# A hybrid layer with 32 experts: the sums of five and six of its modulations as products on TensorE

## The chip, the cores and the metric

The kernel runs on one core of a Trainium2 chip. The metric is the device time of one execution in microseconds (us); lower is better. TensorE (PE in the profile) does matrix products, VectorE (DVE) and ScalarE (ACT) work along the rows of a tile of 128 partitions, GpSimd (POOL) does the same in part, and SyncE (SP) issues transfers from the chip's memory (HBM).

## The reference, cut to what matters

One layer on 256 tokens of width 1024. A conditioning vector `c` gives six vectors of 1024, the modulations; two of them shift and scale the input of the mixers, the third scales the mixers' result, the other three do the same around the experts:

```python
mods = silu(c) @ w_ada + b_ada                 # [1024] @ [1024, 6144], float32
shift1, scale1, gate1, shift2, scale2, gate2 = split(mods, 6)
h = rms_norm(x, norm1_g) * (1 + scale1) + shift1
proj = h @ w_in
y_rwkv = rwkv7_time_mix(proj[..., :RWKV_PROJ], ...)     # 8 heads, recurrent
y_moba = moba_attention(proj[..., RWKV_PROJ:], ...)     # 8 heads, causal
x = x + gate1 * (concat(y_rwkv, y_moba) @ w_out)
h = rms_norm(x, norm2_g) * (1 + scale2) + shift2
y = moe_ffn(h, w_router, ..., w_gate_up, b_gate_up, w_down, b_down)   # top 4 of 32 experts
return x + gate2 * y
```

The expert weights are 32 times 12.58 MB, 403 of the 451 MB that the kernel reads.

## The kernel before, in words

Everything up to the experts is written as threads (generators): the input's norm, the projections, the two mixers, the output projection, the routing, the loads, and `t_mods`, which this change touches. `mix.run` steps them in an order written out by hand as a string of letters (`_ORDER`), one letter per step; a step runs from one `yield` to the next. So the program order on each engine is the order of the steps, and each engine does its instructions in that order. The change leaves the string as it is, and `t_mods` keeps its number of steps.

Weights come in through one list of loads, issued on SP's queue in a fixed order (`_STREAM`), each into a half of one of twelve 2 MB tiles (`take`, `done`, `release`). A load waits in SP's queue until the half that it was given has been read by its former users, and the loads behind it wait with it. `need` gives a thread the half that a load filled, `done` gives it back.

The first two modulations (shift1, scale1) are made earlier on TensorE, at line 557, four column blocks of 512 in four groups of 32 partitions of one PSUM bank (`pa`). `t_mods` makes the other four, in two rounds. Round `g=1` makes gate1 and shift2, `g=2` makes scale2 and gate2. Each round takes eight pieces of w_ada, one per 128 rows of the matrix, 128 partitions by 2048 columns (1 MB). Before, VectorE multiplies each piece by that piece's 128 values of silu(c), one per partition (`sc`), and adds it to an accumulator of 128x2048 (1 MB, half a tile), in two instructions of 1024 columns (lines 1144 and 1146). The 128 partitions are summed at the end by TensorE: `pcol` turns 1024 of the columns into a column layout (line 1154), for s2 at line 1156 and A2 at line 1164, and `pg` spreads the gate over all partitions (line 1185). GpSimd clears the gate's half of the accumulator first (line 1134), and its first partition gets the bias.

Names that follow: `pm`, `pk`, `pr`, `pv`, `plo` are the projections (line 196; line 191 splits a weight for them on VectorE), `px` and `pz` the low-rank parts (686, 706). In the recurrent mixer, `pz2a` and `pz2b` (line 845) and `px2a` and `px2b` (856) are the steps of a triangular solve; between them VectorE evacuates PSUM at lines 848 and 860. `pgu` (line 1395) is the first product of an expert, `pga` (1357) gathers its tokens, `pz` at line 1421 is its second product.

Of the kernel before, what the change touches and what calls it, by code (L numbers as in the profile page):

```python
# [24 lines left out]
AF = mybir.ActivationFunctionType  # L25
ALU = mybir.AluOpType
# [3 lines left out]
D = 1024  # L30
T = 256
KC = 8
# [95 lines left out]
def body(ctx, tc, cst, x, c, w_ada, b_ada, norm1_g, w_in, rwkv_mu, rwkv_w0, rwkv_w_up, rwkv_a0, rwkv_a_up, rwkv_g_up,  # L128
         rwkv_k_k, rwkv_k_a, rwkv_r_k, rwkv_ln_g, rwkv_ln_b, q_norm_g, k_norm_g, w_out, norm2_g, w_router, b_router,
         w_gate_up, b_gate_up, w_down, b_down, out, dbg=None, stop=99):  # L130
    nc = tc.nc
    mm = nc.tensor.matmul
    tr = nc.tensor.transpose
    act = nc.scalar.activation
    V = nc.vector
    G = nc.gpsimd
# [20 lines left out]
    def U(name, wide=False, kind="f"):  # L157
        e = find(wide, kind)
        assert e is not None, (name, [x[1:] for x in live])
        if e == ():  # L160
            nsl[0] += 1
            e = [up.tile([128, 4096], F32, name=f"u{nsl[0]}_" + (name if isinstance(name, str) else "_".join(str(z) for z in name)), tag="u"), kind, [None, None]]
            live.append(e)
        if wide:
            e[2] = [name, name]
            return e[0]
        i = e[2].index(None)
        e[2][i] = name
        return e[0][:, i * 2048:(i + 1) * 2048]

    def release(name):
        for e in live:
            if name in e[2]:
                e[2] = [None if x == name else x for x in e[2]]
                if e[2] == [None, None]:
                    live.remove(e)
                return
        raise KeyError(name)

    def S2(name, dims=None):  # L180
        t = sm.tile([128, 512], F32, name=name, tag="s2", bufs=8)
        return t

    def PB(name):
        return pp.tile([128, 512], F32, name=name, tag="B", bufs=8)
# [16 lines left out]
    def dram(ap, offset, dims):  # L202
        return bass.AP(tensor=ap.tensor, offset=ap.offset + offset, ap=dims)
# [16 lines left out]
    def cc(name, lo=0, n=None):  # L220
        o, w = _CST[name]
        b = o + lo
        e = o + (w if n is None else lo + n)
        return CK[:, b:e] if o < NKEEP else CH[:, b - NKEEP:e - NKEEP]

    ident = cc("ident")
    ones = cc("ones")
# [202 lines left out]
    def pump():  # L430
        while S["wmax"] and S["next"] < len(plan) and fits(S["halves"]) and held[0] + plan[S["next"]][2] <= S["wmax"]:
            load_next()
# [16 lines left out]
    def done(name):  # L449
        t = W.pop(name)  # L450
        if name[0] in ("gu", "dn"):
            held[0] -= 2
            for h in range(2):
                if any((name, h) in e[2] for e in live):
                    release((name, h))
        else:
            held[0] -= 1
            release(name)
        pump()

    def need(name):
        while name not in W or S["next"] < len(plan) and name == plan[S["next"]][0]:
            assert fits(), ("no slot", name, H, list(W))
            load_next()
        return W[name]

    def take(name, kind="f", wide=False):
        assert name not in H
        H.add(name)
        return U(name, wide, kind)  # L470

    def drop(*names):
        for n in names:
            H.remove(n)
            release(n)
        pump()
# [16 lines left out]
    sc = cp.tile([128, KC], F32, name="sc")  # L493
# [17 lines left out]
    def pairs(t, a, r):  # L511

        return t.rearrange("p (a q r) -> p a r q", a=4, r=2)[:, a, r, :]
# [612 lines left out]
    g2z = cp.tile([128, D], F32, name="g2z")  # L1126

    def t_mods():
        GA = None
        for g in (1, 2):  # L1130
            yield "slots", 1
            a = take(f"acc{g}")
            gate = slice((g - 1) * 1024, g * 1024)
            G.memset(a[:, gate], 0.0)
            yield
            nc.sync.dma_start(out=a[0:1, gate], in_=dram(b_ada, (2 if g == 1 else 5) * D, [[D, 1], [1, D]]))
            yield
            for k in range(KC):
                yield "unit", ("ada", g, k)
                w = need(("ada", g, k))  # L1140
                for n in range(2):
                    o = slice(n * 1024, (n + 1) * 1024)
                    if k == 0 and n != g - 1:
                        V.tensor_scalar(a[:, o], w[:, o], sc[:, 0:1], None, op0=ALU.mult)
                    else:
                        V.scalar_tensor_tensor(a[:, o], w[:, o], sc[:, k:k + 1], a[:, o], op0=ALU.mult, op1=ALU.add)  # L1146
                    if n == 0:
                        yield
                done(("ada", g, k))
            yield  # L1150
            ps = PB("pcol")
            o = 1024 if g == 1 else 0
            for k in range(KC):
                mm(ps[:, k:k + 1], pairs(a[:, o:o + 1024], k // 2, k % 2), ones, start=True, stop=True)
            if g == 1:
                V.tensor_tensor(out=s2, in0=ps[:, 0:8], in1=p2[:, 0:8], op=ALU.add)
                GA = a.rearrange("p (a n) -> p a n", a=2)
                E_["g1"] = GA[:, 0]
                for d in range(2):
                    for i in range(2):  # L1160
                        nc.sync.dma_start(out=GA[64 * d + 32 * i:64 * d + 32 * i + 32, 1].rearrange("p (j n) -> p j n", j=2),
                                          in_=dram(b_gate_up, i * 512, [[2 * D, 32], [D, 2], [1, 512]]))
            else:
                V.scalar_tensor_tensor(A2, ps[:, 0:8], 1.0, p2[:, 8:16], op0=ALU.add, op1=ALU.add)
                V.scalar_tensor_tensor(A2, A2, math.sqrt(D), p2[:, 16:24], op0=ALU.mult, op1=ALU.mult)

                tw = S2("tw")[:, 0:KC * NE].rearrange("p (k e) -> p k e", k=KC)
                sw = S2("sw")[:, 0:NE]
                V.tensor_tensor(out=tw, in0=wr, in1=s2[:, :, None].to_broadcast([128, KC, NE]), op=ALU.mult)
                V.tensor_reduce(out=sw, in_=tw.rearrange("p k e -> p e k"), axis=AX.X, op=ALU.add)  # L1170
                V.tensor_tensor(out=wr, in0=wr, in1=A2[:, :, None].to_broadcast([128, KC, NE]), op=ALU.mult)
                bg = cp.tile([128, 1024], F32, name="bgu", tag="bgu")
                E_["bgu"] = bg.rearrange("p (j n) -> p j n", j=2)
                act(bg.bitcast(F32R), GA[:, 1], AF.Copy)
                V.tensor_tensor(out=bg[64:128].bitcast(F32R), in0=GA[64:128, 1], in1=bg[64:128], op=ALU.subtract)
                V.tensor_tensor(out=pick, in0=ident[:, 0:64], in1=ident[:, 64:128], op=ALU.add)
                yield
                ps = PB("psw")
                mm(ps[:, 0:NE], ones.to_broadcast([128, 128]), sw, start=True, stop=True)
                V.tensor_tensor(out=br, in0=ps[:, 0:NE], in1=br, op=ALU.add)  # L1180
            yield
            for n in range(2):
                o = n * 512 if g == 1 else 1024 + n * 512
                ps = PB("pg1")
                mm(ps, ones.to_broadcast([128, 128]), a[:, o:o + 512], start=True, stop=True)
                act(GA[:, 0, n * 512:(n + 1) * 512] if g == 1 else g2z[:, n * 512:(n + 1) * 512], ps, AF.Copy)
                yield
            if g == 2:
                drop("acc2")
            yield "set", f"mod{g}"  # L1190

    def t_out():
# [371 lines left out]
    class Solo:  # L1564
# [6 lines left out]
        def down(self, b, j):  # L1571
# [4 lines left out]
            if j % 4 == 3:  # L1576
                done(("dn", e, j // 4))

    mix.run({"a": t_input(), "b": t_project(), "c": t_mods(), "d": t_rwkv(), "e": t_values(), "f": t_finish(), "g": t_moba(), "h": t_att(0),
             "i": t_att(1), "j": t_out(), "k": t_rank(), "l": t_split(), ".": t_load()}, _ORDER, early)  # L1580
    if stop <= 1:
# [6 lines left out]
    for pair in range(NE // 2):  # L1588
# [6 lines left out]
        for b in range(2):  # L1595
# [4 lines left out]
            t, i, g = XG[e]  # L1600
# [73 lines left out]
    for n in range(2):  # L1674
        for t in range(2):
            ps = PB("pcb")
# [25 lines left out]
```

## Time and profile before

| | us |
|---|---|
| median of 3 runs (lowest, highest) | 1211.56 (1210.47, 1213.37) |
| the profiled execution | 1214.2 |
| its span in the profile | 1212.1 |
| PE busy | 1126.8 (93%) |
| DVE busy | 383.3 (32%) |
| ACT busy | 173.9 (14%) |
| POOL busy | 52.5 (4%) |
| read from HBM | 449.31 MB, 372 GB/s over the span |

The mean granted clock of TensorE is 0.969 of full speed. Busy shares are means over stages with different limits, so the table says little on a change in one stage; the rows below are by stage. Some matmul records can be missing, and the end of a matmul is modelled.

### The profile page before, as it was taken

Reading aid. Unit: us, or ns where it says so; the run is one execution under the profiler, and the core shown is the slowest. Engines: PE = TensorE matmul, PEld = TensorE weight load, DVE = VectorE, ACT = ScalarE, POOL = GpSimd, SP = SyncE. Lnnn points to the kernel's source line nnn. Section 1 sums busy time; section 2 is a strip of 40 time slices with the busy share of each in tenths; the row PEclk is TensorE's granted clock in tenths of the full one; section 3 lists DMA queues with packets and bytes.
Section 4 is the critical chain, followed back from the end, with each engine's and each line's share of the span. In section 5 each row is a group of like instructions: output and inputs, shape, how many; then the busy total and the mean of one; then the engine's idle time right before and its main releaser. Section 6 shows DMA issues by size and latency. Waiting matters only on the chain.

```text
span 1212.1 us, 13675 instructions
## 1 busy us (share of the span) xinstructions
PE 1126.8 (93%) x5769; PEld 495.5 (41%) x5769; DVE 383.3 (32%) x739; ACT 173.9 (14%) x321; POOL 52.5 (4%) x74
## 2 busy tenths in 40 slices
PE   5999888989999999999989998998999899988998
PEld 3776676544433333343234333432343333333332
DVE  2379998552112222220213021212121212111213
ACT  3356354221100000010001000100010000000000
POOL 0002440010000000000000000000000000000000
PEclk9999877998999999999899999999999999999999
DMA  8796573577999999999999999999999999999994
GB/s 284 243 336 237 194 230 121 177 326 312 336 367 417 424 426 429 427 429 425 426 426 429 427 428 428 427 428 427 428 427 428 428 428 428 427 427 428 427 429 203
DMA packets 55436, 451.31 MB, mean 372 GB/s; under 512 B 7738, under 2 KB 17160, under 8 KB 25802
## 3 DMA queue, kind: packets, MB, share of 16 engines
q1 hardware_dynamic: 55082, 449.85, 90.7%
q8 instruction: 48, 0.79, 0.3%
q10 hardware_dynamic: 288, 0.52, 0.1%
q14 instruction: 18, 0.15, 0.0%
HBM read 449.31 MB, written 1.05 MB: 372 GB/s over the span
## 4 chain that ended last, share of the span: by engine, by line
PE 55%; DMA 35%; DVE 7%; issue 1%; ACT 1%; SPq 0%; POOL 0%; ACTq 0%; DVEq 0%; POOLq 0%
PE pgu L1395 22%; PE pz L1421 9%; PE pga L1357 5%; DMA u_('dn', 11, 1)_0_3596<-in_w_down 3%; DMA u_('dn', 19, 1)_0_4783<-in_w_down 3%; DMA u_('dn', 27, 1)_0_5609<-in_w_down 3%; DMA u_('dn', 23, 1)_0_5196<-in_w_down 3%; DMA u_('dn', 15, 1)_0_4370<-in_w_down 3%; DMA u_('dn', 29, 1)_0_5812<-in_w_down 3%; PE pcb L1430 3%; DMA u_('gu', 27, 3)_0_5506<-in_w_gate_up 3%; DMA u_('gu', 11, 3)_0_3483<-in_w_gate_up 3%; DMA u_('gu', 23, 3)_0_5093<-in_w_gate_up 3%; DMA u_('gu', 19, 3)_0_4680<-in_w_gate_up 3%; DMA u_('dn', 7, 1)_0_3169<-in_w_down 2%; DMA u_ada<-in_w_ada 2%
## 5 line engine op out<-in xcount | busy, mean ns | idle before, releaser
L1401 ACT ACTIVATE gt<-gt 128x512 f32<-128x512 f32 x32 | 20.2, 630 | 492.0 <-DVE gt L1400 491.9
L1400 DVE TENSOR_SCALAR gt<-pgu 128x512 f32<-128x512 f32 x32 | 22.1, 692 | 179.3 <-PE pgu L1395 179.3
L1375 DVE COPY ct<-pct 128x256 f32<-128x256 f32 x17 | 7.2, 425 | 222.7 <-PE pct L1374 222.7
L1357 PE MATMUL pga<-oh,u_ada 128*128 128x256 f32 (+1 forms) x288 | 74.6, 382 | 0.4 <-DVE oh L1350 0.2
L1433 DVE TENSOR_TENSOR u_x<-pcb,u_x 128x512 f32<-128x512 f32 x60 | 41.5, 692 | 98.5 <-PE pcb L1430 98.5
L1357 PEld LDWEIGHTS pga<-oh,u_ada 128*128 128x128 f32 x288 | 50.4, 201 | 49.5 <-issue 45.2
L1430 PE MATMUL pcb<-z,ct 128*128 128x512 f32 x120 | 59.5, 618 | 0.0
L1412 ACT ACTIVATE at<-pat 128x512 f32<-128x512 f32 x32 | 19.1, 597 | 230.2 <-PE pat L1410 230.2
L1380 POOL CAST sel<-pick 128x128 fp32r<-128x128 f32 x32 | 9.6, 301 | 853.5 <-PE pz L1421 521.7
L1426 DVE TENSOR_TENSOR z<-pz,g2z 128x512 f32<-128x512 f32 x30 | 20.8, 692 | 74.4 <-PE pz L1421 74.4
L1361 DVE TENSOR_SCALAR u_ada<-pga,A,s 128x256 f32<-128x256 f32 (+1 forms) x24 | 12.0, 499 | 86.3 <-PE pga L1357 86.3
L1430 PEld LDWEIGHTS pcb<-z,ct 128*128 128x128 f32 x120 | 20.3, 189 | 38.7 <-issue 38.7
L1395 PE MATMUL pgu<-u_ada,u_ada 128*64 128x512 f32 x112 | 28.7, 635 | 0.0
L1410 PEld LDWEIGHTS pat<-cst_k,ut 128*128 128x128 f32 x128 | 17.9, 209 | 26.0 <-issue 13.0
L1388 PE MATMUL pgu<-bgu,sel 128*128 128x512 f32 x64 | 25.0, 472 | 2.8 <-PEq L1455 2.8
L196 PE MATMUL pm<-u_wmq,u_hs 128*128 128x512 f32 x96 | 24.9, 415 | 2.3 <-DVE u_wmq L191 2.3
L1359 ACT ACTIVATE u_ada<-pga,s,A 128x256 f32<-128x256 f32 (+1 forms) x24 | 12.7, 528 | 89.7 <-PE pga L1357 89.6
L1402 DVE TENSOR_SCALAR ut<-pgu 128x512 f32<-128x512 f32 x32 | 22.1, 692 | 5.9 <-PE pgu L1395 5.1
L1410 PE MATMUL pat<-cst_k,ut 128*128 128x128 f32 x128 | 23.9, 310 | 0.0
L1403 DVE SCALAR_TENSOR_TENSOR ut<-ut,gt 128x512 f32<-128x512 f32 x32 | 22.2, 692 | 4.7 <-ACT gt L1401 1.2
L196 PEld LDWEIGHTS pm<-u_wmq,u_hs 128*128 128x128 f32 x96 | 18.9, 200 | 7.5 <-DVE u_wmq L191 2.8
L1146 DVE SCALAR_TENSOR_TENSOR u_krg<-u_ada,sc,u_krg 128x1024 f32<-128x1024 f32 x13 | 20.4, 1581 | 0.2
(717 smaller groups left out, 2094.1 us busy)
## 6 DMA issues: line engine op xcount, KB each, us to landing
u_ada<-in_w_gate_up SPq DMA_DIRECT2D x16, 1024.0 KB
u_ada<-in_w_ada SPq DMA_DIRECT2D x13, 1024.0 KB
u_ada<-in_w_ada SPq DMA_DIRECT2D x24, 256.0 KB
u_ada<-in_w_in SPq DMA_DIRECT2D x6, 1024.0 KB
u_sa<-in_w_gate_up SPq DMA_DIRECT2D x5, 1024.0 KB
u_ada<-in_w_down SPq DMA_DIRECT2D x5, 1024.0 KB
u_lo<-in_w_in SPq DMA_DIRECT2D x4, 1024.0 KB
u_vk<-in_w_gate_up SPq DMA_DIRECT2D x3, 1024.0 KB
```

What stands on the lines that cost most here:

```text
L196: mm(out, a[p].bitcast(F32R), b[q_].bitcast(F32R), start=start and i == 0, stop=stop and i == 2, **kw)
L1357: mm(ps[:, 0:n], pairs(xn2[:, t, :], k // 2, k % 2), oh[:, t, 0:n], start=(t == 0), stop=(t == 1))
L1388: mm(ps[a], s_, E_["bgu"][:, a, :].bitcast(F32R), start=True, stop=False, skip_group_check=True)
L1395: mm(ps[a][hs[h], :], xl(k), w[:, a * 1024 + h * 512:a * 1024 + (h + 1) * 512], start=False, stop=(k == KC - 1), skip_group_check=True)
L1400: V.tensor_scalar(gt, ps[0], 7.0, None, op0=ALU.min)
L1402: V.tensor_scalar(ut, ps[1], 7.0, -7.0, op0=ALU.min, op1=ALU.max)
L1403: V.scalar_tensor_tensor(ut, ut, 1.0, gt, op0=ALU.add, op1=ALU.mult)
L1410: tr(pt[:, f * 128:(f + 1) * 128], ut.rearrange("p (q r) -> p r q", r=4)[:, f], ident)
L1421: mm(pz[n][hs[b], :], at[:, j % 4, j // 4, :], w[b][:, n * 512:(n + 1) * 512], start=(j == 0), stop=(j == KC - 1), skip_group_check=True)
L1426: V.tensor_tensor(out=z[i][0:n], in0=pz[i][0:n], in1=g2z[0:n, i * 512:(i + 1) * 512], op=ALU.mult)
L1430: mm(ps[i], ct[0:n, t * 128:(t + 1) * 128], z[i][0:n], start=True, stop=True)
L1433: V.tensor_tensor(out=xs, in0=ps[i], in1=xs, op=ALU.add)
```

## The change

The 32 VectorE instructions and the clearing go. In their place, TensorE multiplies `sc` (one column, repeated 32 times) with 512 columns of the piece, into one of four groups of 32 partitions of one PSUM bank (`pmod`), which is held over all eight pieces; each of the 32 partitions of a group then holds the same sum. The bias is added by two products of one row (`brow`). ScalarE copies the bank to `mrow`, from which the column layout and the spread gate are made, with a column of the identity to choose the group. An accumulator of 1 MB is not needed any more: the first round takes one only after `pcol`, for the gate and the experts' bias, and the second round none.

```diff
--- before.py
+++ after.py
@@ -1126,35 +1126,42 @@
     g2z = cp.tile([128, D], F32, name="g2z")
 
     def t_mods():
-        GA = None
         for g in (1, 2):
-            yield "slots", 1
-            a = take(f"acc{g}")
-            gate = slice((g - 1) * 1024, g * 1024)
-            G.memset(a[:, gate], 0.0)
-            yield
-            nc.sync.dma_start(out=a[0:1, gate], in_=dram(b_ada, (2 if g == 1 else 5) * D, [[D, 1], [1, D]]))
-            yield
+            gate = 0 if g == 1 else 2
+            yield
+            br_ = S2("brow")
+            yield
+            for n in range(2):
+                nc.sync.dma_start(out=br_[32 * n:32 * n + 1], in_=dram(b_ada, (2 if g == 1 else 5) * D + n * 512, [[D, 1], [1, 512]]))
+            yield
+
+            pa = PB("pmod")
             for k in range(KC):
                 yield "unit", ("ada", g, k)
                 w = need(("ada", g, k))
-                for n in range(2):
-                    o = slice(n * 1024, (n + 1) * 1024)
-                    if k == 0 and n != g - 1:
-                        V.tensor_scalar(a[:, o], w[:, o], sc[:, 0:1], None, op0=ALU.mult)
-                    else:
-                        V.scalar_tensor_tensor(a[:, o], w[:, o], sc[:, k:k + 1], a[:, o], op0=ALU.mult, op1=ALU.add)
-                    if n == 0:
+                for i in range(4):
+                    mm(pa[32 * i:32 * i + 32], sc[:, k:k + 1].to_broadcast([128, 32]), w[:, i * 512:(i + 1) * 512], start=(k == 0), stop=(k == KC - 1), skip_group_check=True)
+                    if i == 1:
                         yield
+                if k == 0:
+                    for n in range(2):
+                        i = gate + n
+                        mm(pa[32 * i:32 * i + 32], ones[32 * n:32 * n + 1].to_broadcast([1, 32]), br_[32 * n:32 * n + 1], start=False, stop=False, skip_group_check=True)
                 done(("ada", g, k))
+            mrow = S2("mrow")
+            act(mrow, pa, AF.Copy)
+
+            def row(i):
+
+                return ident[:, 32 * i:32 * i + 1]
             yield
             ps = PB("pcol")
-            o = 1024 if g == 1 else 0
+            o = 2 - gate
             for k in range(KC):
-                mm(ps[:, k:k + 1], pairs(a[:, o:o + 1024], k // 2, k % 2), ones, start=True, stop=True)
+                mm(ps[:, k:k + 1], mrow.rearrange("p (a q r) -> p a r q", a=2, r=2)[:, k // 2 % 2, k % 2, :], row(o + k // 4), start=True, stop=True)
             if g == 1:
                 V.tensor_tensor(out=s2, in0=ps[:, 0:8], in1=p2[:, 0:8], op=ALU.add)
-                GA = a.rearrange("p (a n) -> p a n", a=2)
+                GA = take("acc1").rearrange("p (a n) -> p a n", a=2)
                 E_["g1"] = GA[:, 0]
                 for d in range(2):
                     for i in range(2):
@@ -1180,13 +1187,10 @@
                 V.tensor_tensor(out=br, in0=ps[:, 0:NE], in1=br, op=ALU.add)
             yield
             for n in range(2):
-                o = n * 512 if g == 1 else 1024 + n * 512
                 ps = PB("pg1")
-                mm(ps, ones.to_broadcast([128, 128]), a[:, o:o + 512], start=True, stop=True)
+                mm(ps, row(gate + n).to_broadcast([128, 128]), mrow, start=True, stop=True)
                 act(GA[:, 0, n * 512:(n + 1) * 512] if g == 1 else g2z[:, n * 512:(n + 1) * 512], ps, AF.Copy)
                 yield
-            if g == 2:
-                drop("acc2")
             yield "set", f"mod{g}"
 
     def t_out():
```

Three places in the order of the engines, each before and then changed. The first is TensorE in round one, around 75 us, where `plo` is followed by `px`. Before:

```order
L196 MATMUL plo_178<-u_hs,u_wlo_146 128x256 [waits Activation_49]
L196 MATMUL plo_178<-u_hs,u_wlo_146 128x256 [waits DVE_49]
L196 MATMUL plo_178<-u_hs,u_wlo_146 128x256 x10
L686 MATMUL px_625<-u_hT,u_wm 32x256 [waits DMAHW3_49,PE_49]
L686 MATMUL px_625<-u_hT,u_wm 32x256 x7
L196 MATMUL pk_179<-u_hs,u_wv_456 128x256 x12
```

Changed:

```order
L196 MATMUL plo_178<-u_hs,u_wlo_146 128x256 [waits Activation_49]
L196 MATMUL plo_178<-u_hs,u_wlo_146 128x256 [waits DVE_49]
L196 MATMUL plo_178<-u_hs,u_wlo_146 128x256 x10
L1143 MATMUL pmod<-u_ada_3_0_353,sc 32x512 [waits DMAHW6_49,DMAHW3_49]
L1143 MATMUL pmod<-u_ada_3_0_353,sc 32x512 x3
L686 MATMUL px_635<-u_hT,u_wm 32x256 [waits DMAHW4_49,DVE_49]
L686 MATMUL px_635<-u_hT,u_wm 32x256 x7
L1143 MATMUL pmod<-u_ada_2_579,sc 32x512 [waits DMAHW7_49]
L1143 MATMUL pmod<-u_ada_2_579,sc 32x512 x3
L196 MATMUL pk_179<-u_hs,u_wv_460 128x256 x12
```

Pieces 1 and 2 stand as runs of four on the two sides of `px`, each behind the transfer of its piece, and `px` now waits for VectorE in the place of TensorE itself.

The second place is TensorE in round two, around 180 to 186 us, from the last `pyt` products to `px2a` of the solve. Before:

```order
L827 MATMUL pyt<-cst_k,u_sa 128x64 [waits DVE_49]
L827 MATMUL pyt<-cst_k,u_sa 128x64 x3
L845 MATMUL pz2a<-u_sa,u_xz 64x64 [waits PE_49]
L845 MATMUL pz2a<-u_sa,u_xz 64x64 x7
L845 MATMUL pz2b<-u_sa,u_xz 64x64 x8
L856 MATMUL px2a<-u_xz,u_yg 64x64 [waits DVE_49,Activation_49]
L856 MATMUL px2a<-u_xz,u_yg 64x64 [waits Activation_49]
L856 MATMUL px2a<-u_xz,u_yg 64x64 x6
L856 MATMUL px2b<-u_xz,u_yg 64x64 [waits DVE_49]
```

Changed:

```order
L827 MATMUL pyt<-cst_k,u_ne 128x64 [waits DVE_49]
L827 MATMUL pyt<-cst_k,u_ne 128x64 x3
L845 MATMUL pz2a<-u_ne,u_gb 64x64 [waits PE_49]
L845 MATMUL pz2a<-u_ne,u_gb 64x64 x7
L845 MATMUL pz2b<-u_ne,u_gb 64x64 [waits PE_49]
L845 MATMUL pz2b<-u_ne,u_gb 64x64 x7
L1143 MATMUL pmod<-u_winm_v_848,sc 32x512 [waits DMAHW4_49]
L1143 MATMUL pmod<-u_winm_v_848,sc 32x512
L856 MATMUL px2a<-u_ada_3_1120,u_ne 64x64 [waits DVE_49,Activation_49]
L856 MATMUL px2a<-u_ada_3_1120,u_ne 64x64 [waits Activation_49]
L856 MATMUL px2a<-u_ada_3_1120,u_ne 64x64 x6
```

Two products of piece 6 stand between `pz2b` and `px2a`, behind the transfer of that piece.

The third place is VectorE at the same point of the solve, around 180 to 188 us. Before:

```order
L1119 COPY u_sa<-po 128x256 [waits PE_49]
L1146 SCALAR_TENSOR_TENSOR u_krg_886<-u_ada_5_1153,sc,u_krg_886 128x1024 [waits DVE_49]
L848 TENSOR_TENSOR u_xz<-pz2a,u_x 64x8x32 [waits DVE_49,PE_49]
L848 TENSOR_TENSOR u_xz<-pz2a,u_x 64x8x32 [waits DVE_49]
L848 TENSOR_TENSOR u_xz<-pz2b,u_x 64x8x32 [waits DVE_49,PE_49]
L848 TENSOR_TENSOR u_xz<-pz2b,u_x 64x8x32 [waits DVE_49]
L1146 SCALAR_TENSOR_TENSOR u_krg_886<-u_ada_0_0_131,sc,u_krg_886 128x1024 [waits DMAHW2_49]
L860 TENSOR_TENSOR u_sa<-px2a,u_sa 64x4x16x4 [waits DVE_49,PE_49]
L860 TENSOR_TENSOR u_sa<-px2a,u_sa 64x4x16x4 [waits DVE_49]
```

Changed:

```order
L1119 COPY u_ada_5_821<-po 128x256 [waits PE_49]
L848 TENSOR_TENSOR u_ada_3_1120<-pz2a,u_x 64x8x32 [waits DVE_49,PE_49]
L848 TENSOR_TENSOR u_ada_3_1120<-pz2a,u_x 64x8x32 [waits DVE_49]
L848 TENSOR_TENSOR u_ada_3_1120<-pz2b,u_x 64x8x32 [waits DVE_49,PE_49]
L848 TENSOR_TENSOR u_ada_3_1120<-pz2b,u_x 64x8x32 [waits DVE_49]
L860 TENSOR_TENSOR u_ne<-px2a,u_ne 64x4x16x4 [waits DVE_49,PE_49]
L860 TENSOR_TENSOR u_ne<-px2a,u_ne 64x4x16x4 [waits DVE_49]
```

The product of 128x1024 in front of line 848 and the one behind it are gone, and line 860 follows line 848.

## Rows read from the trace of the kernel before

**Rows 1.** Busy time by window: window, its length, engines busy (instructions), PEclk, DMA share, GB/s.

```profile
60.00:130.00 70.00, 66.46 (x372) 51.19 (x371) 61.90 (x84) 43.47 (x72) 12.51 (x6) 0.98 0.74 266
110.00:120.00 10.00, 7.67 (x29) 5.46 (x27) 9.94 (x13) 4.65 (x9) 3.17 (x2) 0.83 0.38 115
129.00:212.00 83.00, 68.21 (x852) 56.71 (x851) 78.10 (x128) 33.62 (x85) 23.07 (x23) 0.79 0.55 186
180.00:200.00 20.00, 16.37 (x231) 13.69 (x232) 16.85 (x30) 6.22 (x17) 2.71 (x3) 0.74 0.26 67
210.00:250.00 40.00, 36.33 (x446) 22.25 (x444) 22.85 (x56) 9.57 (x23) 3.04 (x3) 0.98 0.46 160
280.00:350.00 70.00, 69.86 (x308) 26.54 (x306) 12.90 (x41) 8.29 (x15) 0.61 (x2) 0.98 0.85 315
350.00:520.00 170.00, 169.79 (x722) 59.05 (x720) 39.70 (x81) 9.85 (x17) 1.78 (x6) 1.00 1.01 424
```

**Rows 2.** Chain that ended last: start, us, what; of 140 to 300 the shares by line.

```profile
98.53 6.93 DMA u_vk<-in_w_ada
...
by line: DVE u_krg L1146 10.1%; PE pgu L1395 9.9%; PE pwo L1208 9.3%; issue 6.9%; PE pwo L1201 6.1%; DVE u_xz L848 4.6%; PE pga L1357 3.7%; PE pw L983 3.4%; DVE u_sa L860 3.1%; PE pg L791 2.5%; PE plg L1268 2.2%; DVE u_ada L1090 1.9%; DVE u
...
184.81 1.12 PE px2a L856 x16
...
192.78 1.07 PE pz2a L845 x16
...
278.88 3.61 PE pgu L1395 x8
...
482.18 25.45 DMA u_('dn', 7, 1)_0_3169<-in_w_down
```

**Rows 3.** Waits of PE, 62 to 129 and 140 to 212: total us, times, longest.

```profile
PE pm L196 <- DVE u_wmq L191: 2.3, 1, 2.3
PE pa L557 <- DMA u_ada<-in_w_ada: 1.2, 1, 1.2
...
PE pqt L1065 <- DVE u_ada L1061: 5.0, 3, 2.6
PE pg L811 <- DVE u_krg L814: 4.4, 1, 4.4
PE px2a L856 <- DVE u_xz L848: 4.2, 3, 2.8
```

**Rows 4.** Groups by shape on DVE, 60 to 130 and 129 to 212: busy, mean ns, idle before.

```profile
L1146 DVE SCALAR_TENSOR_TENSOR u_ada<-u_ada,sc,u_ada 128x1024 f32<-128x1024 f32 x6 | 7.5, 1276 | 0.0
...
L1146 DVE SCALAR_TENSOR_TENSOR u_krg<-u_ada,sc,u_krg 128x1024 f32<-128x1024 f32 x13 | 20.4, 1581 | 0.2
...
L1146 DVE SCALAR_TENSOR_TENSOR u_krg<-u_yg,sc,u_krg 128x1024 f32<-128x1024 f32 x2 | 2.6, 1276 | 0.0
```

**Rows 5.** Timeline of DVE: start us, us, instruction.

```profile
74.86 0.75 DVE L1144 TENSOR_SCALAR u_ada<-u_ada,sc 128x1024 f32<-128x1024 f32 x1
...
128.96 0.17 DVE L1156 TENSOR_TENSOR s<-pcol,p 128x8 f32<-128x8 f32 x1 [0.32 <-PE pcol L1154]
...
180.86 3.02 DVE L1146 SCALAR_TENSOR_TENSOR u_krg<-u_ada,sc,u_krg 128x1024 f32<-128x1024 f32 x1
...
211.31 0.85 DVE L848 TENSOR_TENSOR u_xz<-pz2a,u_x 64x256 f32<-64x256 f32 x2
```

**Rows 6.** Timeline of PE at 42.8, and line 557's products: ns min/median/max.

```profile
42.84 1.06 PE L557 MATMUL pa<-u_ada,sc 128*32 128x512 f32 x8
43.84 1.70 PE L196 MATMUL plo<-u_hs,u_wlo 128*128 128x256 f32 x12
...
L557 PE MATMUL pa<-u_ada,sc x32: 592/604/617, 42.8 to 65.1; 128*32 128x512 f32 x32
```

**Rows 7.** Costliest groups of the page: an ACT copy of 128x512.

```profile
L1412 ACT ACTIVATE at<-pat 128x512 f32<-128x512 f32 x32 | 19.1, 597 | 230.2 <-PE pat L1410 230.2
```

## Prediction, written before the changed kernel ran

> **What bounds the kernel now.** I read the table of busy time by window first, then the chain that ended last, then what TensorE waits for, then VectorE's rows one by one. Four stretches have different limits [rows 1]. From 350 us on the DMA share is 1.01 at 424 GB/s, and the chain there consists of waits for weights, the first at 482.18 for 25.45 us [rows 2]: the end is set by bytes. From 280 to 350 the share is 0.85 at 315 GB/s while TensorE is busy 69.86 of 70 us: the loads wait for halves of tiles that TensorE still reads. So the weight stream runs as early as TensorE lets it, and when the first expert's product starts (278.88, [rows 2]) carries to the end about one for one. The question is therefore by how much the change moves 278.88.
>
> Ahead of that lie two stretches that the change touches. In 60 to 130 TensorE is busy 66.46 of 70 us, VectorE 61.90 [rows 1]; TensorE waits 2.3 us for a VectorE split and 1.2 us for a load, and for nothing else [rows 3]. This is TensorE's stretch, although the chain passes through a load at 98.53 and VectorE behind it [rows 2]. In 129 to 212 VectorE is busy 78.10 of 83 us, TensorE 68.21 at a mean clock of 0.79 [rows 1], and TensorE waits for VectorE 5.0, 4.4 and 4.2 us [rows 3]. This is VectorE's stretch. The change takes work from VectorE in both and gives it to TensorE in both, so I expect a loss in the first and a gain in the second.
>
> **Part 1: what leaves VectorE.** The first modulation (in 60 to 129) has 15 products of 128x1024 at 1.28 us, six of them in the row shown and nine in three rows like it, and one plain product of 0.75: 19.9 us [rows 4, 5]. The second has 20.4 + 2.6 and again 0.75 = 23.7 us [rows 4, 5]; its 13 take 1.58 us on average and not 1.28, because some are stretched, one to 3.02 us [rows 5]. Not all of that is on the path: in the first stretch VectorE has 8 us of idle time and TensorE is the limit, so I give back only what TensorE lost to VectorE: the 2.3 us wait, and 1.7 us from 110 to 120, where the granted clock was 0.83 of full speed for 10 us [rows 1]. In the second, the view that adds up the chain by line has this line at 10.1% of the 160 us from 140 to 300, 16.2 us [rows 2]; that is what I take as on the path, of 23.7.
>
> The memsets on GpSimd (two, and GpSimd is busy 12.5 and 23.1 us in the two stretches [rows 1]) were waited for by nobody in the chain; I cost them at nothing, and their cover is that engine's idle time of some 57 and 60 us.
>
> **Part 2: what TensorE gets.** For each modulation 32 products of 32 columns against 512, plus two of one row for the bias. The first modulation of the layer (line 557) already uses this form: four of them, eight instructions, start at 42.84, and the next product starts at 43.84, so 1.00 us for four; each instruction lasts 592 to 617 ns [rows 6]. After the change the eight pieces of w_ada are cut by the thread's steps: the first place shown from the order has pieces 1 and 2 as whole runs of four, but in the second half of the first modulation four pieces are split into two and two with other products between. I count 12 runs (4 whole, 8 half) there and 13 in the second modulation. What a run of two costs, the trace does not show. Bounds: 0.50 us if cost goes by number, 1.00 if a run lasts as long as one column block's two passes. Since eight instructions of 0.6 us fit in 1.00 us only by lying beside each other, I take 1.00. The bias adds two passes on two of the blocks: between 0 and 1.0, taken 0.9. So 12.9 us (at least 8.5) in the first modulation and 13.9 (at least 8) in the second.
>
> The Trainium skill speaks on this in "TensorE: Matmul & The Clock Gate", Part 3 (packing small matmuls): blocks in different column groups run concurrently, and a pack lasts about as long as one product. By it a run of two saves nothing over a run of four, which gives the 12.9; by the count alone it would be 8.5. A rule in "TensorEngine Tiling (Array Packing)", section Tiling Modes, speaks against the change further: to change the tiling mode drains TensorE, and 25 runs change it 50 times. The row at 42.84 holds one entry and one exit in its 1.00 us and shows no gap at either, so on this trace the rule adds nothing to the sum.
>
> In the first stretch the 12.9 us lie on the limiting engine and count in full. Three things come with them. TensorE takes its work in order, so each load of w_ada that is late now stops the products behind it, where before it stopped only a VectorE sum: SP issues piece 1 only behind a VectorE split, and the accumulator holds one of eight PSUM banks, so that px waits for an evacuation. Bounds: nothing, and the 6.93 us that the load at 98.53 was waited for [rows 2]. I take 2.0, nearer to the 1.2 us row [rows 3]. The new copy of the sums by ScalarE between the last block and pcol: 0.6 us, from the same shape at 597 ns [rows 7]; nothing hides it.
> First stretch: 12.9 + 2.0 + 0.6 - 2.3 - 1.7 = +11.5 us, so that s2, at 128.96 now [rows 5], is written at about 140.5.
>
> In the second stretch the 13 runs lie mostly where TensorE waits for VectorE (the 13.6 us of the three waits), but not all: from 184.81 to 193.8 TensorE holds the chain in eight pieces, the first and the last of them shown [rows 2], and two half runs stand in it (the second place shown from the order). I take 2.5 us as on the path, bounds 0 and 13.9. One load, of piece 4, is issued right behind two others and needed some 8 us later: 0.9, between 0 and the 6.93 of [rows 2]; and the copy 0.6. Against this stands the clock: from 180 to 200 it was 0.74, a loss of 5.2 us in 20 against full speed [rows 1], while TensorE waited for VectorE's 3.02 us product in front of L848. The third place shown from the order has that product gone. With less waiting the clock should stay up for part of it; I take half, 2.6, between 0 and 5.2.
> Second stretch: -16.2 + 2.5 + 0.9 + 0.6 - 2.6 = -14.8 us.
>
> **Part 3: two tiles.** One tile of 1 MB is no longer held at all, the other only from pcol on. It could let weights start earlier. But at 280 us the loads wait for TensorE anyway, and from 210 to 250 the bytes run at 160 GB/s behind halves that w_out and the products hold [rows 1]. 2 MB at 424 GB/s are 4.9 us of stream, worth something only if the stream, not TensorE, sets the start of the experts; I take 0, bounds -4.9 and 0.
>
> **Sum.** +11.5 - 14.8 = -3.3 us at the start of the experts, and the same at the end. The profiled execution took 1214.2 us (2.1 outside its span of 1212.1) and so would take 1210.9. It lies 2.6 above the median of the runs shown, 1211.56; on the median's scale that is 1208.3.
>
> **Rivals.** A, slower: TensorE becomes the limit of the second stretch too. For it: 68.2 us busy plus 13.9 is 82.1 of 83 us. Against: those 68.2 are at a clock of 0.79, and 14 us of idle time are waits for VectorE that go. It decides from about 6 of the 13 runs on the path; with 7 to 13 there, and no gain of the clock, the second stretch gives -7.2 to -0.8 and the whole +4.3 to +10.7; at the middle, +7, about 1218.6.
> B, larger gain: half runs cost half (8.5 instead of 12.9) and the whole 5.2 us of clock comes back: -3.3 - 4.4 - 2.6 = -10.3, about 1201.3. For it: VectorE falls from 78 to 54 us of 83. Against: the concurrency in [rows 6].
> C, no change: the expert stage starts earlier or later but the bytes end at the same time, 1211.6. For it: the chain's long waits for weights from 482.18 on [rows 2]. Against: the 15% idle from 280 to 350, 10 us in which loads wait for TensorE.
>
> **How the numbers follow.** Forecast 0.48 (own range 1204.5 to 1211), A 0.27, B 0.13, C 0.12. A difference under 0.2%, 2.4 us, cannot be told from none. Of the forecast's 0.48 some 0.35 lies beyond that on the fast side, 0.11 within, 0.02 on the slow side. Faster: 0.35 + 0.13 = 0.48; same: 0.11 + 0.12 = 0.23; slower: 0.02 + 0.27 = 0.29. The range 1203 to 1219 leaves out about half of B and a third of A.
>
> **What would show it.** s2 (L1156) at 139 to 142 us: the first stretch is right; under 136: half runs are cheap; over 145: loads stop TensorE, and the waits view will name w_ada with more than 3 us. Row L848 that stood at 211.31 [rows 5] should stand at 207 to 209; over 213 says A. In windows 129 to 212 VectorE should fall to about 54 us of 83 and the clock rise above 0.85. The first L1395 should move from 278.88 by what that row moved, and the chain's first wait for dn 7 as much. The prediction is wrong if those two differ, or if the two stretches do not nearly cancel.

## The result and the profile after

The change moved the sums of four modulations, the third to the sixth, in two rounds. The changed kernel takes 1219.0 us (median of 12 runs, 1213.51 to 1222.88) against 1211.31 (1209.94 to 1213.65) for the kernel before: a ratio of 1.0059, 95% interval 1.0045 to 1.0073, or 7.1 us slower (the medians lie 7.7 apart). The profiled execution took 1216.94 us, with a span of 1214.9. 3.3 us faster was forecast.

The busy time by window of the changed kernel, columns as in [rows 1]:

```profile
60.00:130.00 70.00, 66.60 (x368) 44.01 (x368) 33.01 (x50) 36.93 (x62) 6.87 (x4) 1.00 0.68 243
110.00:120.00 10.00, 10.00 (x45) 5.48 (x45) 4.41 (x9) 8.68 (x13) 6.87 (x4) 1.00 0.27 108
129.00:212.00 83.00, 79.54 (x929) 52.58 (x927) 59.95 (x119) 39.95 (x95) 24.32 (x24) 0.97 0.61 206
180.00:200.00 20.00, 19.98 (x357) 15.29 (x356) 16.18 (x38) 11.17 (x34) 6.72 (x9) 1.00 0.57 151
210.00:250.00 40.00, 37.40 (x473) 25.56 (x473) 21.82 (x54) 10.28 (x23) 2.03 (x2) 0.91 0.38 140
280.00:350.00 70.00, 69.61 (x302) 27.86 (x304) 12.97 (x43) 8.35 (x15) 0.61 (x2) 0.96 0.86 327
350.00:520.00 170.00, 170.00 (x728) 59.28 (x724) 40.10 (x81) 10.25 (x17) 1.78 (x6) 1.00 1.01 425
```

In the first stretch VectorE falls from 61.90 to 33.01 us [rows 1] and TensorE stays full. In the second VectorE falls from 78.10 to 59.95 and TensorE rises from 68.21 to 79.54 of 83 us, at a mean clock of 0.97 in the place of 0.79. So the work moved as it was meant to, and TensorE is nearly full in both stretches. Its waits (total us, times, longest), 60 to 142 and 142 to 215:

```profile
PE pa L557 <- DMA u_ada<-in_w_ada: 1.3, 1, 1.3
PE px L686 <- DVE u_wm L544: 1.2, 1, 1.2
PE pmod L1143 <- DVE u_hs L191: 1.2, 1, 1.2
PE pmod L1143 <- DMA u_ada<-in_w_ada: 0.2, 1, 0.2
...
PE pqt L1065 <- DVE u_ada L1061: 1.6, 1, 1.6
PE pcol L1161 <- ACT mrow L1152: 1.5, 1, 1.5
PE pg L791 <- DVE u_krg L768: 0.3, 1, 0.3
```

The 13.6 us of waits for VectorE in the second stretch [rows 3] are down to 1.9; a new one is pcol, which waits 1.5 us for ScalarE's copy. The chain of work that ended last (start, us, what), first the shares of 140 to 300 us:

```profile
by line: PE pwo L1212 9.3%; PE pgu L1399 8.4%; DMA u_ada<-in_w_ada 6.4%; PE pwo L1205 6.1%; PE pmod L1143 4.4%; PE pga L1361 3.5%; PE pw L983 3.4%; PE pyt L827 3.1%; DVE u_krg L756 2.9%; PE pg L811 2.3%; PE pg L791 2.1%; PE ppt L1106 2.0%; 
...
158.90 10.24 DMA u_ada<-in_w_ada
169.18 1.05 PE pmod L1143 x4
...
209.14 0.49 ACT mrow L1152
209.68 2.41 PE pcol L1161 x16
...
283.05 3.47 PE pgu L1399 x8
```

Where line 1146 stood with 10.1% [rows 2] there is now the load of a piece of w_ada, 10.24 us from 158.90, and TensorE's own products of line 1143. The first expert product, at 278.88 before [rows 2], stands at 283.05. VectorE's timeline (start, us, instruction) gives the stages between, the first, fourth and fifth of the solve's pairs of line 848 among them:

```profile
140.30 0.17 DVE L1163 TENSOR_TENSOR s<-pcol,p 128x8 f32<-128x8 f32 x1 [0.98 <-PE pcol L1161]
...
183.32 0.88 DVE L848 TENSOR_TENSOR u_ada<-pz2a,u_x 64x256 f32<-64x256 f32 x2
...
203.27 0.85 DVE L848 TENSOR_TENSOR u_ada<-pz2a,u_x 64x256 f32<-64x256 f32 x2
...
212.12 0.17 DVE L1171 SCALAR_TENSOR_TENSOR A<-pcol,p 128x8 f32<-128x8 f32 x1 [3.44 <-PE pcol L1161]
...
215.21 0.85 DVE L848 TENSOR_TENSOR u_ada<-pz2a,u_x 64x256 f32<-64x256 f32 x2
```

and the same two pairs of the kernel before:

```profile
175.72 0.86 DVE L848 TENSOR_TENSOR u_xz<-pz2a,u_x 64x256 f32<-64x256 f32 x2
...
201.17 0.85 DVE L848 TENSOR_TENSOR u_xz<-pz2a,u_x 64x256 f32<-64x256 f32 x2
```

With s2 at 128.96 and the fifth pair at 211.31 before [rows 5], the first stretch lost 11.3 us, and the second gave back 7.4 (82.35 to 74.91 us): 46.76 to 43.02 from s2 to the first pair, 25.45 to 19.95 from there to the fourth, and 10.14 to 11.94, a loss, from the fourth to the fifth.

This table has the same stages in every kernel that ran (starts in us of one profiled execution each; "ratio" is to the kernel before on the same chip, with its 95% interval):

| kernel | s2 | first pair | fourth | fifth | first pgu | median us | ratio |
|---|---|---|---|---|---|---|---|
| before | 128.96 | 175.72 | 201.17 | 211.31 | 278.8 | 1211.31 | 1 |
| changed | 140.30 | 183.32 | 203.27 | 215.21 | 283.0 | 1219.00 | 1.0059 (1.0045 to 1.0073) |
| e0 changed, again | 140.96 | 182.72 | 202.67 | 214.26 | 281.6 | 1218.06 | 1.0059 (1.0046 to 1.0072) |
| e1 whole runs | 136.26 | 175.78 | 196.83 | 208.42 | 278.0 | 1213.58 | 1.0020 (1.0008 to 1.0032) |
| e2 round 2 only | 127.38 | 169.86 | 190.88 | 202.47 | 271.2 | 1205.08 | 0.9953 (0.9936 to 0.9970) |
| e3 round 1 only | 140.67 | 187.26 | 210.71 | 220.84 | 289.6 | 1222.80 | 1.0101 (1.0077 to 1.0125) |
| e4 thin round 2 | 140.88 | 182.37 | 202.56 | 215.41 | 284.1 | 1219.91 | 1.0067 (1.0048 to 1.0086) |
| e5 thin round 1 | 134.05 | 176.32 | 197.20 | 208.77 | 277.5 | 1212.13 | 0.9999 (0.9985 to 1.0014) |
| e6 round 2, whole | 127.81 | 167.73 | 188.08 | 199.78 | 267.8 | 1202.76 | 0.9921 (0.9901 to 0.9941) |
| e7 VectorE thin | 126.29 | 166.65 | 186.50 | 195.54 | 262.5 | 1199.16 | 0.9897 (0.9871 to 0.9922) |
| e8 e6, copy on VectorE | 126.67 | 166.81 | 188.04 | 198.30 | 266.2 | 1200.80 | 0.9927 (0.9914 to 0.9940) |
| e9 changed, halves held | 140.25 | 183.33 | 203.61 | 215.55 | 283.3 | 1219.31 | 1.0079 (1.0065 to 1.0093) |
| e10 e6, again | 128.43 | 169.72 | 190.36 | 201.95 | 270.7 | 1203.40 | 0.9932 (0.9917 to 0.9948) |
| e11 e8, again | 128.74 | 168.64 | 188.81 | 199.06 | 268.6 | 1201.44 | 0.9922 (0.9906 to 0.9938) |
| e12 e8, loads 4, 5, 6 | 127.59 | 167.51 | 188.25 | 198.50 | 265.6 | 1201.11 | 0.9917 (0.9903 to 0.9932) |
| e13 e7, loads 4, 5, 6 | 127.50 | 165.58 | 185.53 | 194.57 | 261.6 | 1197.01 | 0.9890 (0.9872 to 0.9908) |
| e14 changed, loads 4, 5, 6 | 141.09 | 183.80 | 204.11 | 215.79 | 283.8 | 1220.28 | 1.0083 (1.0060 to 1.0106) |
| e15 e4, loads 4, 5, 6 | 141.65 | 178.05 | 198.10 | 211.09 | 278.2 | 1212.89 | 1.0017 (1.0003 to 1.0032) |

One profiled execution can be some us off its kernel's median: the profile of before (1214.2) lies 2.9 us above its median, that of the changed kernel 2.1 below. With round 1 on VectorE s2 stands at 126.3 to 129.0 in nine profiles (mean 127.7), with it whole on TensorE in half runs at 140.3 to 141.7 in seven (mean 140.8; e1 and e5 left out). So the first stretch costs nearer 13.1 us than 11.3; and with the second stretch's mean of 74.6 in the changed kernel, e0, e9 and e14, against 81.3 in before and e3, the two add up to 13.1 - 6.7 = 6.4 of the 7.1 us.

### The profile page after: what moved, and what is told of

It is laid out like the page before. It is cut to its first block, busy times and chain, and to the rows that moved or that the text cites. A ratio compares the mean times of both kernels' runs of the same rounds, so it can differ in the third digit from the quotient of the medians.

```text
span 1214.9 us, 13918 instructions
## 1 busy us (share of the span) xinstructions
PE 1143.0 (94%) x5905; PEld 487.7 (40%) x5905; DVE 341.1 (28%) x707; ACT 174.6 (14%) x323; POOL 47.2 (4%) x72
## 3 DMA queue, kind: packets, MB, share of 16 engines
HBM read 449.31 MB, written 1.05 MB: 371 GB/s over the span
## 4 chain that ended last, share of the span: by engine, by line
PE 59%; DMA 36%; DVE 3%; ACT 1%; issue 0%; POOL 0%; SPq 0%; ACTq 0%; DVEq 0%; POOLq 0%
PE pgu L1399 22%; PE pz L1425 10%; PE pga L1361 5%; DMA u_('dn', 11, 1)_0_3645<-in_w_down 3%; DMA u_('dn', 29, 1)_0_5861<-in_w_down 3%; DMA u_('dn', 15, 1)_0_4419<-in_w_down 3%; DMA u_('dn', 19, 1)_0_4832<-in_w_down 3%; DMA u_('dn', 23, 1)_0_5245<-in_w_down 3%; DMA u_('dn', 25, 1)_0_5452<-in_w_down 3%; DMA u_('dn', 27, 0)_0_5605<-in_w_down 3%; DMA u_('gu', 29, 3)_0_5741<-in_w_gate_up 3%; PE pcb L1434 3%; DMA u_('gu', 11, 3)_0_3532<-in_w_gate_up 3%; DMA u_('gu', 19, 3)_0_4729<-in_w_gate_up 3%; PE pm L196 2%; DMA u_('gu', 15, 3)_0_4316<-in_w_gate_up 2%
## 5 line engine op out<-in xcount | busy, mean ns | idle before, releaser
L1392 PEld LDWEIGHTS pgu<-bgu,sel 128*128 128x128 f32 x64 | 10.3, 193 | 21.8 <-issue 21.5
L1143 PE MATMUL pmod<-u_ada,sc 128*32 128x512 f32 x80 | 17.3, 603 | 1.4 <-DVE u_hs L191 1.2
```

Source lines behind the costliest of these rows:

```text
L1392: mm(ps[a], s_, E_["bgu"][:, a, :].bitcast(F32R), start=True, stop=False, skip_group_check=True)
```

## Experiments

**The changed kernel again, and either round alone (e0, e2, e3).** `t_mods` takes each round's old or new code by a switch:

```diff
         for g in (1, 2):
+            te = g in TE_G          # (2,) in e2, (1,) in e3
...
+            if te:                  # the changed kernel's lines
...
+            else:                   # the lines of the kernel before
...
```

e0: 

> The changed kernel once more, for a second profile beside a measured spread. Theory (TensorE is the limit of both stretches, and what it loses to the granted clock now counts in full): 1216 to 1222 us, with runs several us apart, and in each run the longer time goes with the lower mean granted clock; L848's fifth pair at 213 to 219 us. Rival (the loss is a fixed cost of waits for w_ada): runs within 3 us of each other whatever the clock.

e2: 

> Round 1 on VectorE as in the kernel before, round 2 on TensorE as in the changed one. Theory (the loss is TensorE's 12 runs in the first stretch, the second stretch gains 7 us): s2 at 129 as before, L848's fifth pair near 204 to 206 us, the time 1203 to 1206 us. Rival (in the second stretch the gain comes only from the late start of the recurrent mixer's solve, which gives TensorE time to run ahead; from a start at 129 the products of round 2 are on TensorE's path): fifth pair at 209 to 212, 1209 to 1213 us.

e3: 

> Round 1 on TensorE as in the changed kernel, round 2 on VectorE as in the kernel before. Theory (11 us lost in the first stretch and nothing gained in the second): s2 at 140, L848's fifth pair at 220 to 223 us, the time 1219 to 1224 us. Rival (the start at 140 is made up in the second stretch whatever round 2 does, since VectorE had fallen behind there): fifth pair at 213 to 216, 1212 to 1216 us.

e0 measured 1218.06 us, 1216.11 to 1218.84. In the 12 runs of the result the time falls by 0.8 us for each 0.001 of mean granted clock (correlation -0.82), but in e0's own six by 0.34 (-0.93), much as in 17 runs of before (0.33, -0.69); and e0's six lie within 2.7 us, as the rival had it. So longer time goes with lower clock in both kernels, and that a loss of clock costs the changed kernel more is not shown. e2 is 1205.08 us: round 2 on TensorE gains by itself, 0.47%, and 75.09 us from s2 to the fifth pair is what the changed kernel has. e3 is 1222.80: round 1 on TensorE loses by itself, 1.0%. Both rivals fall. The two rounds are two changes of opposite sign, and they add up: -0.47 and +1.01 give 0.54% against the 0.59% of the whole.

**What the first stretch pays for (e1, e5).** e1 puts the step's border ahead of a piece's first product, e5 makes the products of pieces 1 to 7 narrow (32 columns of 512, so that the sums are incomplete, while the order stays):

```diff
                 for i in range(4):
+                    if i == 0:                        # e1
+                        yield
-                    mm(pa[32 * i:32 * i + 32], ..., w[:, i * 512:(i + 1) * 512], ...)
+                    nw = 32 if g == 1 and k else 512  # e5; g == 2 in e4
+                    mm(pa[32 * i:32 * i + 32, 0:nw], ..., w[:, i * 512:i * 512 + nw], ...)
-                    if i == 1:                        # e1
-                        yield
...
```

e1: 

> The changed kernel with the four products of every piece in one step of the thread, so 8 runs of four per round in the place of 12 and 13 runs. Theory (a run of two costs as much as a run of four, 1.0 us, and TensorE is the limit in both stretches): 4 us less in the first stretch (s2 at 136 instead of 140.3), up to 5 less in the second, together 1210 to 1214 us. Rival (cost by number of products): s2 stays at 140 and the time at 1217 to 1221.

e5: 

> The same for round 1: the products of its pieces 1 to 7 on 32 columns. Theory (the 11 us of the first stretch are TensorE's runs): s2 at 130 to 132 us in the place of 140.3, the time 1207 to 1211 us. Rival (they are waits for w_ada and for px's PSUM bank): s2 at 136 to 140, 1214 to 1219 us.

In e1 s2 comes at 136.26, 4.5 us below the mean of 140.8, for four runs less; the time is 1213.58. In the changed kernel's own timeline of TensorE a run of four, the bias, and then a half run (x4, four instructions) each end where the next product starts:

```profile
70.72 1.07 PE L1143 MATMUL pmod<-u_ada,sc 128*32 128x512 f32 x8 [1.19 <-DVE u_hs L191]
71.72 1.05 PE L1149 MATMUL pmod<-brow,cst_k 1*32 1x512 f32 x4
72.70 3.13 PE L196 MATMUL pv<-u_hs,u_wv 128*128 128x256 f32 x24
...
92.94 1.05 PE L1143 MATMUL pmod<-u_ada,sc 128*32 128x512 f32 x4
93.92 1.42 PE L196 MATMUL pm<-u_wv,u_hs 128*128 128x512 f32 x5
```

70.72 to 71.72 is 1.00 us for eight instructions, 92.94 to 93.92 is 0.98 for four. So cost does not go by number. In e5 s2 comes at 134.05, 6.8 us below the mean and not the 8 to 10 that were expected, and the time is 1212.13: at least half of the first stretch's 13.1 us is the runs of pieces 1 to 7. What stays with narrow products is the first piece and the bias (70.72 to 72.70, 2.0 us), some 0.2 us for each narrow run, and waits. The waits are 2.6 us in the changed kernel (shown above: 1.2 for px, 1.2 and 0.2 for pmod) and 3.3 in e5, where that of px has grown to 2.2, so part of what the runs gave up went into it. The rival, that it is waits, holds for 2.6 us of the loss. The copy ahead of pcol costs nothing here: ScalarE makes it at 134.71 in 0.58 us, while TensorE has other products until pcol:

```profile
133.34 1.05 PE L1143 MATMUL pmod<-u_winm_v,sc 128*32 128x512 f32 x4
...
138.33 1.93 PE L1161 MATMUL pcol<-cst_k,mrow 128*128 128x1 f32 x16
```

**What the second stretch pays for (e4, e7).** e4 is e5's edit in round 2. e7 is the kernel before with round 2's VectorE instructions narrow for pieces 1 to 7:

```diff
-                        o = slice(n * 1024, (n + 1) * 1024)
+                        o = slice(n * 1024, n * 1024 + (32 if g == 2 and k else 1024))
```

e4: 

> The changed kernel, with the products of pieces 1 to 7 in round 2 on 32 columns of 512 (the sums are left incomplete): all waits and the order stay, the time of TensorE's products goes. Theory (the runs of round 2 stand on the path, some 9 of 13.9 us): the stretch from s2 to L848's fifth pair, 73 to 75 us in the changed kernel, falls to 64 to 67, the time to 1208 to 1212 us. Rival (the forecast's 2.5 us on the path was right, and the second stretch gave little because the 16.2 us of VectorE were not on the path): the stretch stays at 71 to 74, the time at 1215 to 1218 us.

e7: 

> The kernel before, with VectorE's instructions for pieces 1 to 7 of round 2 on 32 columns of 1024 (the sums are left incomplete), and nothing added on TensorE: what VectorE's time in the second stretch is worth by itself. Theory (the chain's 16.2 us on the path were right): the stretch from s2 to the fifth pair falls from 82.4 to 64 to 67 us, the time to 1194 to 1198 us. Rival (the recurrent mixer's own chain limits it): the stretch at 72 to 75, the time 1202 to 1205 us.

e4 missed: nothing came back (1219.91 us, 74.53 from s2 to the fifth pair). Its TensorE timeline shows why, with the narrow products of pieces 3 and 4:

```profile
164.62 0.25 PE L1160 MATMUL pmod<-u_ada,sc 128*32 128x32 f32 x4
168.56 0.32 PE L1160 MATMUL pmod<-u_ada,sc 128*32 128x32 f32 x4 [3.69 <-DMA u_ada<-in_w_ada]
168.81 1.98 PE L811 MATMUL pg<-u_krg,u_ada 128*64 128x128 f32 x16
```

TensorE now waits 3.69 us for the load of piece 4, and `pg` behind it starts at 168.81 in the place of 170.16. e7 missed too: 13.1 us come back (82.35 to 69.25; 10.9 against e3's 80.17, where round 2 is the same), between theory and rival. Piece 0 and the narrow instructions, of 0.25 us each as a rule, are still there, but line 1172, which holds them, has only 1.3 us of e7's chain. The chain names the same load:

```profile
145.28 10.52 DMA u_ada<-in_w_ada
```

**The load of piece 4 (e13 to e15, and e12).** SP issues pieces 6, 5, 4 of round 2 in this order, all three when the half that piece 6 gets has been given back; piece 4 is used first and comes last (issued at 158.03, 158.42 and 158.90 in the changed kernel, right behind TensorE's run on piece 0, which ends at 158.00 in the chain). The edit swaps two entries of the list of loads:

```diff
-..., 55, 56, 61, 60, 59, 39, ...
+..., 55, 56, 59, 60, 61, 39, ...
```

e13: 

> VectorE's round 2 on 32 columns as before, and the loads of its pieces 4, 5, 6 issued in that order, where all others issue 6, 5, 4. Theory (once VectorE's time is gone the load of piece 4, third of three and 10.5 us in the chain, is what ends last, and this is why the forecast's 16.2 us did not come back): s2 to L848's first pair 36 to 38 us against 40.4, the time 1195 to 1197.5 against 1199.2. Rival (the mixer's own chain is what is left): no change, 1198 to 1200.

e14: 

> The changed kernel with its loads of pieces 4, 5, 6 in that order. Theory (there TensorE's runs end at the same moment as that load, so that either alone changes nothing): 0 to 1.5 us less, 1216.5 to 1219. Rival (the load alone sets it): 3 to 5 us less, 1213 to 1215.5.

e15: 

> Both together in the changed kernel: round 2's products of pieces 1 to 7 on 32 columns, and the loads in order 4, 5, 6. Theory: the wait of 3.7 us for piece 4 goes and the runs too, s2 to L848's first pair 37 to 39 us against 41.5 and 43, the time 1212.5 to 1215.5. Rival (neither is on the path): 1217 to 1220.

e14, the swap alone, changes nothing (1220.28). e4, the narrow products alone, changed nothing. e15, both together, takes s2 to the first pair from 43.02 to 36.40 us and the time to 1212.89:

```profile
141.65 0.17 DVE L1193 TENSOR_TENSOR s<-pcol,p 128x8 f32<-128x8 f32 x1 [0.98 <-PE pcol L1189]
...
178.05 0.86 DVE L848 TENSOR_TENSOR u_ada<-pz2a,u_x 64x256 f32<-64x256 f32 x2
```

So in the changed kernel the runs and the load stand beside each other and end within 0.2 us of one another (the run of piece 4 starts at 169.18, right behind the one before it; the load, 158.90 + 10.24, lands at 169.14), and each hides the other. This decides what e4 left open.

In e13 the swap gives 2.2 us more (69.25 to 67.07), and no load of w_ada is left in its chain: with the load out of the way, VectorE's round 2 was worth at least 15.3 us (13.1 against e3). It is a lower end, since line 1172 still has 5.7 us of that chain (8.2% of 126 to 196), among them three narrow instructions:

```profile
152.50 2.58 DVE u_krg L1172 x3
```

These are single profiles, and two of one kernel differ by 1.6 us in this stretch (e6 71.97, e10 73.52); the times of e7 and e13 have overlapping intervals.

**The two halves (e9).** 

> The changed kernel, with both accumulator halves taken and held as before, without being used for sums. Theory (the two halves freed are worth nothing, since TensorE and not the stream sets the start of the experts): 1217 to 1220 us. Rival (they let the weights start earlier): up to 4.9 us longer, 1220.5 to 1224 us.

```diff
+                yield "slots", 1
+                a = take(f"acc{g}")
...
```

1219.31 us, ratio 1.0079 against 1.0059 with overlapping intervals, and the first expert product at 283.3 against 283.0: the halves are worth nothing that can be measured.

**A better version (e6, e8, e10 to e12).** Round 1 on VectorE, round 2 on TensorE in whole runs; e8 has the copy of the sums on VectorE.

e6: 

> The best guess at a better version: round 1 on VectorE, round 2 on TensorE with each piece in one run of four. Theory (8 runs in the place of 13 in a stretch that TensorE limits): the stretch from s2 to the fifth pair 71 to 73 us against 75.1 with half runs, the time 1201 to 1203.5 us. Rival (in round 2 the half runs fill gaps, and a whole run holds up the solve's products longer): 1205 to 1208 us.

e8: 

> The version with round 1 on VectorE and round 2 on TensorE in whole runs, with the copy of round 2's sums from PSUM on VectorE in the place of ScalarE. Theory (behind the last run the copy waits for ScalarE's three instructions of line 1100, and VectorE then stands idle for 3.1 us until pcol; VectorE is free there): 1 to 1.5 us earlier at the A2 instruction, 1201 to 1202.5 us against 1202.8. Rival (the solve's products, not A2, set the fifth pair): no difference, 1202 to 1203.5 us.

```diff
-            act(mrow, pa, AF.Copy)
+            V.tensor_copy(mrow, pa)
```

e6 is 1202.76 us (0.9921), 2.3 below e2, with intervals that just overlap, so the gain is likely and not shown. In the changed kernel ScalarE's copy stands behind line 1100 (ScalarE's timeline; the last run ends at 207.4):

```profile
207.65 1.49 ACT L1100 ACTIVATE u_ada<-u_ada 128x128 f32<-128x128 f32 x4 [0.60 <-DVE u_ada L1097]
209.05 0.57 ACT L1152 ACTIVATE mrow<-pmod 128x512 f32<-128x512 f32 x1
```

In e8 VectorE copies as soon as the run ends, and the A2 instruction follows:

```profile
192.37 0.69 DVE L1178 COPY mrow<-pmod 128x512 f32<-128x512 f32 x1
...
195.20 0.17 DVE L1200 SCALAR_TENSOR_TENSOR A<-pcol,p 128x8 f32<-128x8 f32 x1 [1.73 <-PE pcol L1188]
```

Fourth to fifth pair is 10.26 us in e8 and 11.70 in e6. Whether this carries to the end the ratios did not tell, so both ran once more on one chip.

e10: 

> Round 1 on VectorE, round 2 on TensorE in whole runs, copy on ScalarE, once more, to stand beside the next one on one chip: 1201 to 1204 us.

e11: 

> The same with the copy of round 2's sums on VectorE. Theory (the 1.4 us that A2 comes earlier carry to the end): 1.0 to 1.8 us less than the kernel beside it. Rival (they are made up behind): within 0.5 us of it.

e11 is 1201.44 us against 1203.40, 2.0 less; the intervals of the ratios overlap, so it is likely and not shown. e12, with the load order on top: 

> Round 1 on VectorE, round 2 on TensorE in whole runs with the copy on VectorE, loads in order 4, 5, 6. Theory (runs and load end together here as well): 1199.5 to 1201.5 us. Rival (with whole runs TensorE waits for that load): 1197 to 1199.5 us.

1201.11 us: no change, so the load by itself costs nothing there. It does not stand in e8's chain either; in its place stands the transfer of the bias row, which the bias products behind piece 0 wait for:

```profile
137.97 6.45 DMA brow<-in_b_ada
```

What an earlier transfer of it would give was not tried. The fastest kernels with complete sums are thus e8 (with e11, the same kernel) and e12, some 9 to 10 us (0.7 to 0.8%) below the kernel before.

## Why the prediction was wrong, by its own steps

- **The bound, and the end following the first expert product: right.** From that product to the end of the span it is 930.4 to 934.0 us in all 18 rows of the table, over starts from 261.6 to 289.6. (Before: 1212.1 - 278.8 = 933.3.)
- **First stretch, +11.5: right, a little small.** 11.3 in the pair of profiles, 13.1 over all. A half run costs 0.98 us, where 1.00 was taken, and there are 12 runs as counted; waits 2.6, where 2.0 was taken. The copy, 0.6, was hidden by TensorE's other products, though the prediction said that nothing hides it; the two errors cancel. The clock and the VectorE wait that were to come back, 4.0, came back (clock 1.00 from 110 to 120).
- **Second stretch, -14.8: this step failed.** 7.4 us were measured in the pair of profiles, 6.7 over all, so the two stretches did not cancel. Three terms of its sum were mis-sized:
  - VectorE on the path, 16.2, and the clock on top, 2.6, together 18.8. Measured by e7: 13.1, the clock's part within it, and 14.4 if the 1.3 us that line 1172 keeps in its chain counted in full. The share of a line in the chain says how often it ended last, not what is late next: here the load of piece 4, which held back some 2 us (e13). Whether all of the 18.8 would have come back without it stays open, since what e13 gives, 13.1 to 15.3, is a lower end.
  - The runs on the path, 2.5, and the load, 0.9. The 2.5 was placed in the solve, and there the runs cost nothing: from first to fourth pair 19.95 us in the changed kernel, 19.85 in e7, and 20.05 in e15 with narrow runs. Ahead of the solve, where none were put on the path, they cost 1.4 to 2.7 us above e7, but 5.4 to 6.6 above e15: runs and load are one cost with two causes, and the sum treated them as two small ones.
  - The copy, 0.6. From the fourth to the fifth pair it is 11.94 and 11.59 us in the changed kernel and e0, 9.04 in e7: 2.6 to 2.9. The copy itself takes 0.57; what was left out is that it is queued behind ScalarE's line 1100, and VectorE's A2 and what hangs on it behind pcol, in front of the fifth pair. With the copy on VectorE 1.3 to 1.4 us of it come back (e8 against e6, e11 against e10).
  Their sum by the runs, -13.1 + 1.4 to 2.7 + 2.6 to 2.9, is -9.1 to -7.5; the two profiles of the changed kernel have -7.4 and -9.05.
- **Rival A** had the sign, the price (+7) and half of the mechanism; by the prediction's own sign, a fifth pair over 213, it is A (215.21). TensorE is nearly full, 79.54 of 83 us, and once the load is moved its runs are what ends last: from s2 to the first pair 42.71 us in e14, 36.40 in e15. But as the kernel stands they share the place with the load (e4 took them away and gained nothing), and the clock, which A left without a gain, rose from 0.79 to 0.97. That its +7 is the measured difference is in part luck. **B** fell with the half run's 0.98 us, although its clock came back (1.00 from 180 to 200); **C** fell with the 930.4 to 934.0 us that follow the first expert product.
- **Two halves freed, 0: right**, as far as e9 can tell.
- The Trainium skill's rule on packs ("TensorE: Matmul & The Clock Gate", Part 3: a pack lasts about as long as one product) agrees with 1.00 us for four and 0.98 for two: the single product of line 1191, also against 512 columns, stands with 1.05 us in the changed kernel's chain (at 223.93). The drain that the Trainium skill states for a change of tiling mode ("TensorEngine Tiling (Array Packing)", Tiling Modes) shows no gap here either: the product behind the bias at 71.72 starts at 72.70.

## What to carry to other kernels

A line's share of the chain is not what its removal gives: before it goes into a sum, ask which load, queue or engine is late next at that place, and test it with the instructions made narrow rather than removed, remembering that narrow ones still cost something. Two causes that end at the same moment each show no effect alone, so a null result for one of them clears neither. And a change that acts in two stages with different limits is two changes: judge each by itself, here one of +12 us (e3) and one of -6 us (e2).

## What the runs showed of the hardware

A run of two column blocks of 32 costs TensorE as much as a run of four, 0.98 against 1.00 us for products of 512 columns in float32, so a pack split over two places paid nearly its whole price twice.
